# The second batch's column of token 512: its two rounded parts from ScalarE instead of VectorE

## The chip, the cores and the metric

The kernel runs on one core of one Trainium2 chip. The metric is the device time of the whole kernel in microseconds (us). An execution is compared with others of the same kernel and with the kernel before; the profile is one further execution, recorded by the hardware profiler.

The engines are called TensorE (PE in the profile; PEld is its weight load), VectorE (DVE), ScalarE (ACT), GpSimd (POOL) and SyncE (SP, which here only issues transfers). Each works through its own queue of instructions in order.

## The reference

One encoder layer is applied to two batches of 1024 tokens by 1024 channels (`x_prompt` and `x_sample`, in the kernel batch 0 and batch 1). What matters here is its first branch: the normalized input is projected, and a Fourier transform over the tokens and over the 256 channels of each group follows.

```python
def encoder_layer(x, g_pre, w_in, ...):
    xn = rmsnorm(x, g_pre)
    p = xn @ w_in
    fv, fg, hv, hg, mg = jnp.split(p, [...], axis=-1)
    fz = fv.astype(jnp.float32).reshape(B, L, F_GROUPS, F_GROUP_DIM)
    fz = jnp.fft.fftn(fz, axes=(1, 3), norm="ortho").real
    fz = fz.reshape(B, L, F_WIDTH).astype(dt)
    y_f = (fz * jax.nn.silu(fg)) @ w_fourier_out
    ...
    out = (g_f * y_f + g_h * y_h) @ w_out
    return x + rmsnorm(out, g_post)
```

The rest is a convolution branch with filters that are computed in the frequency domain, two gates and an output projection.

## The kernel before

All large products are made in a split form. An fp32 operand is stored as two rounded parts: a high part (a copy that rounds to the type fp32r) and a low part (the operand less its high part, rounded in the same way). A product is then three matmuls, high by high, high by low and low by high (`mm3`, L465). The helper `split` (L167) makes both parts: the high part on ScalarE or VectorE (L170, L172), the low part as a subtraction on VectorE or GpSimd (through `sub` and `tt`, L180).

The Fourier stage uses the symmetry of the transform: each token column is folded into sums and differences of token t and token 1024 - t. Tokens 0 and 512 are their own mirror images. Token 512 is kept apart, in a small tile `x5` of 128 partitions by 8 channel tiles by 36 columns; for batch b its high part goes to columns b and b + 32, its low part to columns b + 2 and b + 34. TensorE multiplies `x5` with the folded projection weights into a tile of 36 rows (`pfx`, in `fourier_half`).

The two batches come to this stage in different ways. Batch 0 is handled two channel tiles at a time (`two_tiles`), and the two parts of its column are made once for all eight tiles. Batch 1 is handled tile by tile in `xtile`, for k from 0 to 7. Tile k is loaded (`xk`, three buffers, from SyncE's queue), transposed and scaled by eight matmuls with a diagonal matrix into two PSUM tiles (`tpx`, from a ring of four that the projection's `pfv` shares), drained by ScalarE into the tile `xg` (L437, two buffers), and stored to DRAM (`d_x`, L438, the same queue as the loads). Then come the sums (`eo[:, 0]`, VectorE) and differences (`eo[:, 1]`, GpSimd) of the fold, their high part `eh` (ScalarE) and low part `el` (VectorE), and the two parts of token 512's column, both on VectorE. `xg` has two columns behind its 1024 tokens, which a memset on GpSimd (L431) clears.

While `xtile` runs for batch 1, the transform of batch 0's second half is still being made on the same engines (`fourier_half`: the tiles `pse`, `pso`, `sst`, `pp`, `qp`, `pP`, `pQ`, `fPs`, `fPm`, `fA`, `fB`); the projection of batch 1 (`pfv`, `pfx`) follows. Behind the Fourier stage comes the filter stage (`phase_main`), in which the weights of the gates' projections are rounded half a block at a time: loaded to `wr`, high part `wh` on ScalarE, low part `wl` on GpSimd, and used by the matmuls into `pin`.

The order of each engine's queue isn't that of the source. A scheduler builds it from the source's instructions by simulating them against a cost model, so that a small change of the source can move instructions far from it.

Of the kernel before, what the change touches and what calls it, by code (L numbers as in the profile page):

```python
# [9 lines left out]
F32 = mybir.dt.float32  # L10
F32R = mybir.dt.float32r
I32 = mybir.dt.int32
AF = mybir.ActivationFunctionType
# [3 lines left out]
P = 128  # L17
# [143 lines left out]
class K:  # L161
# [262 lines left out]
    def xtile(self, b, k, px, fo):  # L424


        nc, a = self.nc, self.a
        xt = px.tile([P, 8, P], F32, tag="x", name=f"xk{b}_{k}", bufs=3)
        nc.sync.dma_start(xt, a[f"x{b}"].rearrange("(m p) c -> p m c", p=P)[:, :, k * P:(k + 1) * P])
        xg = px.tile([P, L + 2], F32, tag="xg", name=f"xg{b}_{k}", bufs=2)  # L430
        nc.gpsimd.memset(xg[:, L:L + 2], 0.0)  # L431
        for n in range(2):
            tp = self.psum("mm", 4, "tpx")
            for q in range(4):
                m = 4 * n + q
                self.mm(tp[:, q * P:(q + 1) * P], xt[:, m], self.diag[:, m], True, True)
            nc.scalar.activation(xg[:, 512 * n:512 * n + 512], tp, AF.Copy, scale=self.gpre[:, k:k + 1])  # L437
        nc.sync.dma_start(self.d_x[b][k], xg[:, 0:L])  # L438
        eo = px.tile([P, 2, 2, 256], F32, tag="eo", name="eo", bufs=2)
        fw = xg[:, 0:512].rearrange("p (a r) -> p r a", r=2)  # L440
        bw = xg[:, 1024:512:-1].rearrange("p (a r) -> p r a", r=2)
        self.add("dve", eo[:, 0], fw, bw)
        self.sub("pool", eo[:, 1], fw, bw)
        self.split(fo["eh"][:, k], fo["el"][:, k], eo, "dve", "act")
        x5 = fo["x5"][:, k]
        self.split(x5[:, b:b + 33:32], x5[:, 2 + b:35 + b:32], xg[:, 512:513].to_broadcast([P, 2]), "dve", "dve")


    def open_weights(self, pw):
# [1133 lines left out]
```

## Time and profile before

| what | value |
| --- | --- |
| median of three runs | 2414.27 us (2414.0 to 2417.5) |
| the profiled execution | 2412.46 us, of which span 2410.7 us |
| mean granted TensorE clock | 0.998 |
| columns of batch 1 (`xtile`) | about 104 to 142 us |
| filter stage | about 202 to 660 us |

The span is the time from the profile's first instruction to its last. A row of the profile names a source line, an engine, an operation, the tiles written and read (buffer numbers left out), the shape, and how often; in a list of instructions in order of time the first two numbers are start and duration in us, and a bracket at the end holds the idle time of the engine before it and what ended it. In a list of groups the numbers behind the bar are busy us, mean ns of one, and idle us before them with what ended most of it. A row of a list of waits reads: engine, tile and line that waited, what for, us in total, times, longest. Where one tile's instructions are listed, three durations in ns are the shortest, the median and the longest. Durations of neighbours on one engine overlap a little at their ends.

### The profile page before, as it was taken

The numbers are of one execution on the slowest core, as the hardware profiler recorded it, in microseconds if no ns is written. First come the engines' busy times: TensorE is split into PE (matmuls) and PEld (weight loads), VectorE is DVE, ScalarE is ACT, GpSimd is POOL, SyncE is SP. The second block draws the span as 40 slices with busy tenths as digits, with TensorE's granted clock in tenths as the row PEclk, the third lists the DMA queues.
The fourth block names the chain that finished last, engine by engine and source line by source line (L and its number), as shares of the span: only waits on it lengthen the run. The fifth ranks groups of instructions, "written<-read, shape, count | busy, mean of one in ns | idle before, by whom it ended". The sixth has DMA issues, their size and how long they took to land.

```text
span 2410.7 us, 36396 instructions
## 1 busy us (share of the span) xinstructions
PE 2368.0 (98%) x13000; PEld 2056.8 (85%) x13000; DVE 1903.5 (79%) x3393; ACT 1073.0 (45%) x2038; POOL 509.2 (21%) x526
## 2 busy tenths in 40 slices
PE   6999999999999999999999999999999999999998
PEld 5998888888888888888888888888888888888886
DVE  7876988888759999999889999867555456665677
ACT  6646666677533333333223223333444444444443
POOL 3341222222242334441000000112100111212111
PEclk9999999999999999999999999999999999999999
DMA  8636655555555455545444444445454667776543
GB/s 262 213 127 220 212 174 170 168 166 162 189 189 183 158 187 175 172 155 195 148 131 140 131 149 135 136 131 184 162 166 157 206 214 256 252 262 216 162 158 131
DMA packets 228464, 428.33 MB, mean 178 GB/s; under 512 B 23286, under 2 KB 89176, under 8 KB 228026
## 3 DMA queue, kind: packets, MB, share of 16 engines
q1 hardware_dynamic: 200493, 333.03, 43.0%
q0 software_dynamic: 27568, 92.94, 11.2%
q8 instruction: 102, 1.67, 0.3%
q14 instruction: 80, 0.66, 0.1%
q10 hardware_dynamic: 221, 0.04, 0.0%
HBM read 290.12 MB, written 135.79 MB: 177 GB/s over the span
## 4 chain that ended last, share of the span: by engine, by line
PE 53%; DVE 0%; DMA 0%; issue 0%; DVEq 0%; ACT 0%; ACTq 0%
PE pin L193 16%; PE pg L193 8%; PE pyh L193 7%; PE pyf L193 7%; PE po L193 6%; PE pT L193 4%; PE pX L193 4%; PE tph L895 1%; DMA wh<-d_w 0%; DVE o L176 0%; DVE xl L180 0%; DVE yc L180 0%; DVE t L180 0%; DVE rs_t L246 0%; DVE rs L247 0%
## 5 line engine op out<-in xcount | busy, mean ns | idle before, releaser
L193 PE MATMUL pin<-xh,wl 128*128 128x512 f32 x1472 | 576.3, 392 | 1.6 <-POOL wl L180 1.6
L193 PE MATMUL pin<-xh,wh 128*128 128x512 f32 x1472 | 576.1, 391 | 1.5 <-DMA wh<-d_w 1.2
L193 PE MATMUL pin<-xl,wh 128*128 128x512 f32 x1472 | 576.4, 392 | 1.1 <-DVE xl L180 0.9
L180 POOL TENSOR_TENSOR wl<-wr,wh 128x512 fp32r<-128x512 f32 x136 | 251.9, 1853 | 1142.0 <-ACT wh L170 1092.3
L193 PEld LDWEIGHTS pin<-xh,wh 128*128 128x128 f32 x1472 | 277.0, 188 | 55.0 <-DMA wh<-d_w 2.1
L193 PEld LDWEIGHTS pin<-xl,wh 128*128 128x128 f32 x1472 | 277.0, 188 | 54.0 <-DVE xl L180 2.2
L193 PEld LDWEIGHTS pin<-xh,wl 128*128 128x128 f32 x1472 | 277.0, 188 | 53.8 <-POOL wl L180 2.6
L170 ACT CAST wh<-wr 128x512 fp32r<-128x512 f32 x264 | 163.5, 619 | 321.7 <-PE pin L193 94.9
L193 PE MATMUL pX<-bh,cfwd 128*128 128x256 f32 x768 | 161.9, 289 | 0.2 <-DVE t L180 0.2
L180 DVE TENSOR_TENSOR t<-pX,k 128x1024 f32<-128x1024 f32 x128 | 155.4, 1214 | 5.6 <-PE pX L193 3.7
L180 DVE TENSOR_TENSOR wl<-wr,wh 128x512 fp32r<-128x512 f32 x128 | 88.0, 687 | 91.0 <-ACT wh L170 90.7
L193 PE MATMUL pyf<-sf,wh 128*128 128x512 f32 x512 | 157.5, 389 | 0.0
L193 PE MATMUL pyh<-sh,wh 128*128 128x512 f32 x512 | 157.2, 389 | 0.0
L193 PE MATMUL pT<-cinv,yh 128*128 128x256 f32 x768 | 145.6, 284 | 0.0
L170 ACT CAST bh<-b 128x512 fp32r<-128x512 f32 x144 | 88.8, 620 | 112.1 <-DVE b L180 77.5
L193 PEld LDWEIGHTS pX<-bh,cfwd 128*128 128x128 f32 x768 | 126.6, 190 | 2.8 <-DVE t L180 0.6
L193 PEld LDWEIGHTS pT<-cinv,yh 128*128 128x128 f32 x768 | 123.1, 190 | 6.7
L170 ACT CAST yh<-y 128x512 fp32r<-128x512 f32 x96 | 59.5, 620 | 138.8 <-DVE y L180 136.3
L193 PEld LDWEIGHTS pyh<-sh,wh 128*128 128x128 f32 x512 | 96.1, 188 | 19.9
L193 PEld LDWEIGHTS pyf<-sf,wh 128*128 128x128 f32 x512 | 96.1, 188 | 19.8
L193 PE MATMUL pT<-cinv,yl 128*128 128x256 f32 x384 | 109.4, 285 | 0.1
L193 PE MATMUL pX<-bl,cfwd 128*128 128x256 f32 x384 | 108.7, 283 | 0.6 <-DVE bl L180 0.6
(374 smaller groups left out, 5313.4 us busy)
## 6 DMA issues: line engine op xcount, KB each, us to landing
k<-d_k SPq DMA_DIRECT2D x128, 512.0 KB, 4.1
wr<-in_w_in SPq DMA_DIRECT2D x136, 256.0 KB, 3.1
d_g<-gt SPq DMA_DIRECT2D x124, 256.0 KB, 2.7
d_k<-kt SPq DMA_DIRECT2D x128, 128.0 KB, 2.2
d_k<-kt SPq DMA_DIRECT2D x64, 256.0 KB, 2.4
wr<-in_w_fo POOLq DMA_DIRECT2D x64, 256.0 KB, 4.1
g<-d_g SPq DMA_DIRECT2D x64, 256.0 KB, 4.0
wr<-in_w_ho POOLq DMA_DIRECT2D x64, 256.0 KB, 3.7
```

What stands on the lines that cost most here:

```text
L170: self.rounded = nc.scalar.copy(h, src)
L180: return e.tensor_tensor(out, a, b, op=op)
L193: return self.nc.tensor.matmul(out, lhsT, rhs, start=start, stop=stop, skip_group_check=shared)
L895: nc.tensor.transpose(tp[:, q * P:(q + 1) * P], eo[:, e, q], self.ident)
```

## The change

In `xtile`, the call of `split` with both parts on VectorE becomes two instructions of ScalarE: a copy that rounds (the high part), and an activation with the function Identity, a scale of -1 and the column as its bias, which gives the column less the high part and rounds it (the low part). Each writes two columns of 128 partitions, as before. Nothing else is edited.

```diff
         self.split(fo["eh"][:, k], fo["el"][:, k], eo, "dve", "act")
         x5 = fo["x5"][:, k]
-        self.split(x5[:, b:b + 33:32], x5[:, 2 + b:35 + b:32], xg[:, 512:513].to_broadcast([P, 2]), "dve", "dve")
+        hi = x5[:, b:b + 33:32]
+        nc.scalar.copy(hi, xg[:, 512:513].to_broadcast([P, 2]))
+        nc.scalar.activation(x5[:, 2 + b:35 + b:32], hi.bitcast(F32), AF.Identity, bias=xg[:, 512:513], scale=-1.0)
```

VectorE's queue has 16 instructions fewer (3379 for 3395 in the program), ScalarE's 16 more (2010 for 1994); the other three queues hold the same instructions. In the scheduled program the order differs from TensorE's 666th to its 3717th matmul, and on the other engines over the corresponding part; before and behind it is the same.

## The prediction

> **What bounds the kernel now.** I read the page's busy times first, then the list of waits for TensorE over the whole span, then the stretch in which the edited lines run.
>
> ```profile
> span 2410.7 us, 36396 instructions
> PE 2368.0 (98%) x13000; PEld 2056.8 (85%) x13000; DVE 1903.5 (79%) x3393; ACT 1073.0 (45%) x2038; POOL 509.2 (21%) x526
> ```
>
> TensorE (PE) is busy for 98% of the span. The change gives it no work and takes none from it, so the time can move only through its idle time, 2410.7 - 2368.0 = 42.7 us in all, or through its clock. The edited lines run once for each of the eight column tiles of the second batch, between 104 and 142 us. The next fence has the table of stretches (PE, PEld, DVE, ACT and POOL busy with their counts, then granted clock, DMA share, GB/s) and TensorE's waits in the first stretch and in the other two.
>
> ```profile
> 104.00:142.00 38.00, 34.29 (x277) 33.55 (x276) 35.20 (x61) 24.09 (x40) 19.96 (x16) 0.96 0.70 236
> 142.00:202.00 60.00, 59.88 (x493) 58.51 (x492) 37.47 (x98) 23.45 (x60) 18.13 (x22) 1.00 0.35 120
> 202.00:660.00 458.00, 455.56 (x2513) 395.92 (x2512) 388.69 (x871) 314.27 (x672) 115.00 (x69) 1.00 0.57 181
> ...
> PE tpx L193 <- DMA xk<-in_x: 2.1, 1, 2.1
> PE pQ L193 <- DVE qp L180: 1.1, 1, 1.1
> PE pfv L193 <- ACT xg L437: 0.6, 1, 0.6
> ...
> PE pin L193 <- POOL wl L180: 1.6, 2, 0.9
> ```
>
> From 104 to 142 us TensorE loses 38.00 - 34.29 = 3.71 us, in the three waits of the list; VectorE (DVE) is the busiest engine beside it, 35.20 of 38.00. From 142 to 202 us TensorE has no wait worth naming. In the filter stage, 202 to 660 us, it loses 2.4 us, of which 1.6 us are two waits for GpSimd (POOL).
>
> **What is removed.** Sixteen VectorE instructions on 128x2 elements, a cast and a subtraction for each tile.
>
> ```profile
> L180 DVE TENSOR_TENSOR x<-xg,x 128x2 fp32r<-128x2 f32 x8 | 6.2, 779 | 0.0
> L172 DVE CAST x<-xg 128x2 fp32r<-128x2 f32 x8 | 3.9, 489 | 0.0
> ...
> 114.22 1.95 DVE L180 TENSOR_TENSOR eo<-xg 128x512 f32<-128x512 f32 x1
> 116.09 1.48 DVE L172 CAST x<-xg 128x2 fp32r<-128x2 f32 x1
> 117.60 0.16 DVE L180 TENSOR_TENSOR x<-xg,x 128x2 fp32r<-128x2 f32 x1
> 117.68 0.69 DVE L180 TENSOR_TENSOR qp<-sst,qp 128x514 fp32r<-128x514 f32 x1
> 118.28 0.69 DVE L180 TENSOR_TENSOR eo<-xg 128x512 f32<-128x512 f32 x1
> ...
> 121.68 1.46 DVE L180 TENSOR_TENSOR x<-xg,x 128x2 fp32r<-128x2 f32 x1
> ```
>
> ```profile
> 113.51 0.10 POOL L431 MEMSET xg<- 128x2 f32 x1 [2.71 <-DMA d_x<-xg]
> 113.57 3.97 POOL L180 TENSOR_TENSOR eo<-xg 128x512 f32<-128x512 f32 x2
> ```
>
> They hold VectorE for 6.2 + 3.9 = 10.1 us, far more than two elements a lane need. The cast at 116.09 ends at 117.57, where GpSimd ends its pair of subtractions `eo` (113.57 + 3.97 = 117.54); the next operation of the same shape, at 117.60, takes 0.16 us. So most of that time is VectorE held off until GpSimd is done. It isn't a property of the small operations: the 128x512 `eo` at 114.22 took 1.95 us where the one at 118.28 took 0.69. In the changed order of VectorE the instruction behind `eo` is again one with both inputs in SBUF (px, qp, el) behind tiles 0, 1, 2, 4, 5 and 6, and inherits the hold; only behind tiles 3 and 7 is it a drain of PSUM. I count as freed the own work, 16 x 0.16 us = 2.6 us, and the holds of those two tiles (1.46 - 0.16 us at 121.68, and as much again): 5 of the 10.1 us.
>
> The Trainium skill (SBUF — State Buffer, section "Who interferes with whom") says that a VectorE instruction with two SBUF inputs and a GpSimd instruction that reads SBUF exclude each other for a whole instruction. By it the hold goes to the next such instruction in the queue, which speaks against the change; the 1.95 us above agree. Taken for every instruction behind `eo`, it would keep tile 3's 1.46 us too and make the sum 0; the section exempts an instruction with a single SBUF input, as the drains of PSUM are, and with that it is the sum below.
>
> **What is added.** Sixteen ScalarE instructions on 128x2. The trace has the nearest row at the same shape, the copy of L362.
>
> ```profile
> L362 ACT COPY r<-xg x8: 190/193/207, 23.4 to 54.9; 128x2 f32<-128x2 f32 x8
> 122.90 0.36 ACT L577 COPY fPs<-pP 128x256 f32<-128x256 f32 x1
> 115.70 0.49 ACT L578 ACTIVATE fPm<-pP,vec 128x258 f32<-128x258 f32 x1
> ```
>
> The copy costs 0.19 us. The activation with a bias at this shape isn't in the trace: at least 0.19 us, at most the 0.49 us of L578's activation on 258 columns; I take 0.20, as it is nearer in shape. That makes 8 x (0.19 + 0.20) = 3.1 us, at most 5.4 us, in a stretch where ScalarE is idle for 38.00 - 24.09 = 13.9 us. No table load is added in the changed order. Without that cover, each pair would put 0.4 us before an eviction of `xg`.
>
> **What is late next.** The longest of the three waits decides.
>
> ```profile
> 115.57 0.34 SPq L438 DMA_DIRECT2D d_x<-xg  x1
> 116.00 0.46 SPq L429 DMA_DIRECT2D xk<-in_x  x1
> ...
> 122.32 0.69 ACT L437 ACTIVATE xg<-tpx,gpre 128x512 f32<-128x512 f32 x1 [2.18 <-DMA d_x<-xg]
> ...
> 118.42 0.51 PE L193 MATMUL pQ<-qp,chan 128*128 128x258 f32 x2 [1.09 <-DVE qp L180]
> ...
> 123.84 3.24 PE L193 MATMUL tpx<-dg,xk 128*128 128x128 f32 x16 [2.05 <-DMA xk<-in_x]
> ...
> q1 hardware_dynamic: 4991, 4.85, 97.1%
> ```
>
> TensorE waits until 123.84 for the load of tile 6, issued at 116.00. The store of tile 2, issued 0.43 us ahead of it in the same queue, landed only at 122.32, 6.75 us after its issue, and from 112 to 128 us (the fence's last row, from the DMA queues of that stretch) this queue's packets fill 97.1% of the DMA engines. The load is held by transfers, not by VectorE. The wait of 1.09 us for `qp`, ahead of it, goes: GpSimd's next `eo` now stands behind the memset of tile 3, which waits for a store of tile 1 as that of 113.51 did for tile 0's, so `qp` is free to run behind `eo`, at about 114.22 + 1.95 = 116.2. But TensorE only reaches tile 6 earlier and waits there longer. Worth 0, bounds 0 and -1.09 us.
>
> SyncE's queue itself sees one delay. Tile 2's second eviction now stands behind the two drains of pP (0.36 + 0.49 = 0.85 us), so that tile's store and the load of tile 6 are issued up to 0.85 us later. Bounds 0 and +0.85 us; I take 0, as the queue has two older transfers under way. Tile 7's load is issued about 1 us earlier and lands no sooner, for the same reason.
>
> Then the wait of 0.57 us ahead of the first `pfv`:
>
> ```profile
> 125.96 5.12 POOL L180 TENSOR_TENSOR eo<-xg 128x512 f32<-128x512 f32 x2 [0.73 <-DVE x L172]
> ...
> 129.04 1.05 ACT L170 CAST eh<-eo 128x1024 fp32r<-128x1024 f32 x1 [0.66 <-DVE x L180]
> ...
> 130.26 1.27 ACT L437 ACTIVATE xg<-tpx,gpre 128x512 f32<-128x512 f32 x2
> ...
> 128.49 1.95 PE L193 MATMUL tpx<-dg,xk 128*128 128x128 f32 x16
> 131.01 0.51 PE L193 MATMUL pfv<-we,eh 128*128 128x260 f32 x2 [0.57 <-ACT xg L437]
> ```
>
> `pfv` needs a PSUM buffer that ScalarE drains at 130.26, behind the cast `eh` of 129.04, which waits for tile 4's `eo`. GpSimd starts that one at 125.96, after VectorE's `el` of tile 2 has freed its buffer. Without the 1.46 us of tile 3 ahead of it, that `el` runs some 1.5 us earlier, the chain follows, and the drain comes at about 129 us, ahead of the end of TensorE's `tpx` (128.49 + 1.95 = 130.44). The wait goes: -0.57 us. TensorE is bound by its own work behind it, so the gain carries on to the end.
>
> **Further on.** The list of instructions differs in its order on every engine up to TensorE's 3717th matmul of 12584, near 650 us, and is the same behind that. In the filter stage instructions of VectorE move by about ten places and the rounding of weights on ScalarE by up to 19. I counted, for each of the 60 weight halves of this stage, TensorE's work between the last matmul for which ScalarE's queue up to their rounding waits and their first use, with 0.23 us from matmul to matmul:
>
> ```profile
> 689.71 0.39 PE L193 MATMUL pin<-xh,wh 128*128 128x512 f32 x1
> 689.93 0.39 PE L193 MATMUL pin<-xl,wh 128*128 128x512 f32 x1
> ```
>
> 8 halves of before, and 10 of after, have less than 8 us. With the slack alike I take 0 for this part, bounds -1.6 (both waits gone) and +6.4 us (rival 4).
>
> **The sum.** 0 - 0.57 + 0 + 0 = -0.57 us. The profiled execution took 2412.46 us, 1.76 us beside its span, and would take 2411.9; the median of the runs, 2414.27, lies 1.8 us above it, so the forecast there is 2413.7 us, with 2412.6 to 2414.6 as its own range (the bounds -1.09 and +0.85 us above).
>
> **The rivals.** 1. VectorE's freed 5 us come through: tile 6 lands earlier, since stores leave earlier, and all three waits and the slow clock behind them go.
>
> ```profile
> 122.00:124.00 2.00, 0.16 (x1) 0.19 (x2) 2.00 (x4) 1.68 (x4) 1.16 (x2) 1.00 0.95 288
> 124.00:126.00 2.00, 2.00 (x12) 2.00 (x12) 2.00 (x5) 2.00 (x4) 0.14 (x2) 0.60 0.80 278
> 126.00:128.00 2.00, 2.00 (x12) 2.00 (x11) 2.00 (x3) 0.63 (x2) 2.00 (x1) 0.55 0.90 311
> ```
>
> After the idle stretch the granted clock is 0.60 and 0.55 for 4 us, which costs 4.00 - 2.00 x (0.60 + 0.55) = 1.70 us. All together -(1.09 + 2.05 + 0.57 + 1.70) = -5.4: 2408.9 us. The full DMA queue speaks against it.
>
> 2. The clock keeps up: the idle time now comes in two pieces (tile 5's load, then tile 6's), and the dip stays away: -0.57 - 1.70 = -2.3: 2412.0 us.
>
> 3. The clock drops once more or for longer and tile 6 comes 0.85 us later: -0.57 + 0.85 + 1.70 = +2.0: 2416.3 us. The Trainium skill (TensorE: Matmul & The Clock Gate, section "What's actually happening") has the clock halved after an idle window of about 3.4 us that runs free of the program; by it rivals 2 and 3 hang on where the window falls, each at 1.70 us for a window won or lost, and the 4 us here agree.
>
> 4. The slower side: the new order starves GpSimd's rounding of weights in the filter stage.
>
> ```profile
> L180 POOL TENSOR_TENSOR wl<-wr,wh 128x512 fp32r<-128x512 f32 x136 | 251.9, 1853 | 1142.0 <-ACT wh L170 1092.3
> ...
> 456.71 5.43 POOL L180 TENSOR_TENSOR wl<-wr,wh 128x512 fp32r<-128x512 f32 x1 [8.46 <-ACT wh L170]
> ```
>
> A `wl` that meets a run of VectorE's two-input work takes up to 5.43 us where the page's mean is 1.853. Two waits cost 1.6 us, 0.8 each; if all ten tight halves waited so, 8.0 - 1.6 - 0.57 = +5.8: 2420.1 us. It decides from one further wait on (0.8 against 0.57). Against it: of the 60 halves of before, 8 of them tight, two waited.
>
> 5. The change does nothing in the end: the drain at 130.26 stays where it is, as the added instructions in ScalarE's queue take back what VectorE gives. 2414.3 us.
>
> **How the numbers follow.** Forecast 0.37, rival 1 0.10, rival 2 0.12, rival 3 0.15, rival 4 0.18, rival 5 0.08. About 0.2%, 4.8 us, is what a measurement of this kernel tells from no change. Beyond it on the fast side lies rival 1 and a little of rival 2: 0.11. On the slow side most of rival 4 and a little of rival 3: 0.15. Within: 0.74. The range goes from rival 1 to rival 4, 2409 to 2420 us.
>
> **What would show it.** Right: no `x` of VectorE between 104 and 142 us; the copies at 0.19 us and the activations at about 0.2; `qp` of 117.68 near 116.2; TensorE still waits for tile 6 until 122.3 to 124.7; the first `pfv` at about 130.5 with no wait; two or three waits for `wl`. Wrong: tile 6 started before 122 us (rival 1), a granted clock of 1.00 from 124 to 128 us (2) or below it for over 5 us (3), four or more waits for `wl` in the filter stage (4), and above all a difference that arises behind 660 us, where the orders agree and I allow nothing.

## The result, and the profile after

The changed kernel takes 2417.85 us (median of 21 runs, 2414.58 to 2421.62), the kernel before, run beside it, 2412.92 us (21 runs, 2409.43 to 2417.96). The ratio is 1.0020, with a 95% interval from 1.0015 to 1.0026: the change costs some 4.9 us, where 0.57 us of gain was forecast. The profiled execution of the changed kernel took 2414.58 us, its fastest, so its profile can't show all of the loss.

The page of the changed kernel, span and busy times:

```profile
span 2412.8 us, 36397 instructions
PE 2368.4 (98%) x13000; PEld 2057.6 (85%) x13000; DVE 1895.1 (79%) x3377; ACT 1075.4 (45%) x2054; POOL 503.9 (21%) x526
```

TensorE is as busy as before (2368.4 us for 2368.0). Its table of stretches (columns as in the prediction) tells where its idle time lies:

```profile
104.00:142.00 38.00, 35.35 (x293) 34.06 (x292) 33.55 (x51) 27.70 (x60) 17.40 (x18) 1.00 0.69 240
142.00:202.00 60.00, 59.85 (x492) 58.49 (x491) 35.94 (x94) 23.73 (x60) 18.57 (x21) 1.00 0.40 136
202.00:660.00 458.00, 450.91 (x2482) 392.11 (x2482) 385.64 (x869) 312.41 (x669) 112.52 (x67) 1.00 0.55 178
```

In the stretch that holds the edited lines TensorE is idle for 38.00 - 35.35 = 2.65 us, 1.06 us less than before, and its clock is 1.00 where it was 0.96. In the filter stage, where nothing is edited, it is idle for 458.00 - 450.91 = 7.09 us; before it was 2.44, so 4.65 us are lost there.

That a gain of 1.06 us, a clock dip of 1.70 us that stays away and a loss of 4.65 us add up to +1.9 us, near the two spans' difference of 2.1 us, is partly chance, as these terms aren't all. The changed kernel has a dip of its own in the filter stage: the granted clock is 0.79, 0.50 and 0.86 in the three stretches of 2 us from 212 to 218 us, which costs 1.70 us again; in the kernel before it is 1.00 there. The filter stage can also be timed as a whole, from the first matmul into `pin` (at 202.08 us before, 200.50 after) to the first one from which on TensorE's order is the same again (657.02 and 660.98 us). It lasts 460.48 us instead of 454.94, 5.54 us more. The changed kernel comes to it 1.58 us sooner, and takes 1.85 us less behind it.

The list of TensorE's waits for the whole span names what it waited for there (total, times, longest):

```profile
PE pin L193 <- POOL wl L180: 3.1, 1, 3.1
PE tpx L193 <- DMA xk<-in_x: 2.4, 4, 1.3
PE pin L193 <- ACT xh L170: 1.6, 1, 1.6
...
PE pXf L193 <- ACT kt L806: 1.4, 1, 1.4
```

The filter stage has one long wait for GpSimd's `wl` instead of two short ones, and two waits for ScalarE, for `xh` and `kt`. The list of instructions in order of time shows the first of the three, on VectorE, GpSimd and TensorE of the changed kernel:

```profile
249.52 0.27 DVE L764 TENSOR_SCALAR T<-T,vec 128x128 f32<-128x128 f32 x1
249.72 0.68 DVE L180 TENSOR_TENSOR xp<-fE 128x512 f32<-128x512 f32 x1
...
257.22 0.75 DVE L180 TENSOR_TENSOR b<-xm,bs 128x256 f32<-128x256 f32 x2
258.32 1.32 DVE L180 TENSOR_TENSOR bl<-b,bh 128x512 fp32r<-128x512 f32 x1 [0.35 <-ACT bh L170]
...
250.68 10.12 POOL L180 TENSOR_TENSOR wl<-wr,wh 128x512 fp32r<-128x512 f32 x2 [1.18 <-ACT wh L170]
...
259.15 0.50 PE L193 MATMUL pin<-xh,wl 128*128 128x512 f32 x1 [3.15 <-POOL wl L180]
```

The view of the tile `wl` between 244 and 265 us gives the shortest, median and longest of three, in ns:

```profile
L180 POOL TENSOR_TENSOR wl<-wr,wh x3: 1292/1730/8418, 245.0 to 259.1; 128x512 fp32r<-128x512 f32 x3
```

The `wl` that starts at 250.68 takes 8.418 us. In that time VectorE runs additions and subtractions of two inputs in SBUF without a break, from 249.72 until it waits 0.35 us for a `bh`, ahead of 258.32. The `wl` ends at 250.68 + 8.42 = 259.10, which is 1.13 us behind the beginning of that gap (258.32 - 0.35 = 257.97), and TensorE goes on at 259.15. In the kernel before, the scaling of T stood inside such a run:

```profile
250.99 2.60 POOL L180 TENSOR_TENSOR wl<-wr,wh 128x512 fp32r<-128x512 f32 x1
...
252.36 1.31 DVE L762 TENSOR_SCALAR T<-T,vec 128x128 f32<-128x128 f32 x1
```

There the `wl` ended at 253.59, 1.23 us behind the start of the scaling. In the changed order the scaling (L764, the same instruction) is done at 249.52, ahead of the run and of the `wl`.

The other two waits are for ScalarE. The rows of ScalarE, and TensorE's two waits, in the changed kernel:

```profile
207.97 1.28 ACT L747 ACT_TABLE_LOAD   x1
209.26 1.71 ACT L747 ACTIVATE ex<-dec,vec 128x256 f32<-128x256 f32 x4
210.88 1.03 ACT L170 CAST xh<-xl 128x1024 fp32r<-128x1024 f32 x1
...
369.56 1.28 ACT L882 ACT_TABLE_LOAD   x1
...
372.47 0.31 ACT L806 ACTIVATE kt<-kt 128x128 f32<-128x128 f32 x1
...
211.96 0.51 PE L193 MATMUL pin<-xh,wh 128*128 128x512 f32 x1 [1.63 <-ACT xh L170]
...
372.84 0.36 PE L193 MATMUL pXf<-bh,cfwd 128*128 128x256 f32 x1 [1.43 <-ACT kt L806]
```

A table load and four `ex` stand ahead of the `xh` that TensorE wants, and a table load ahead of the `kt`. For the `kt` this is new: from 360 to 374 us the kernel before loads a table once, the changed kernel three times. For the `xh` it isn't. In the kernel before the same load and the same `ex` stand ahead of it, and it runs later, but TensorE has 18 matmuls (into `pft` and `pQ`) between its `pP` at 211.34 and the matmul that needs the `xh`; in the changed order that matmul comes directly behind `pP`. The kernel before:

```profile
213.49 1.03 ACT L170 CAST xh<-xl 128x1024 fp32r<-128x1024 f32 x1
...
214.57 1.02 PE L193 MATMUL pin<-xh,wh 128*128 128x512 f32 x2 [0.28 <-ACT xh L170]
```

### The profile page after: what moved, and what is told of

It is laid out like the page before. It is cut to its first block, busy times and chain, and to the rows that moved or that the text cites. A ratio compares the mean times of both kernels' runs of the same rounds, so it can differ in the third digit from the quotient of the medians.

```text
span 2412.8 us, 36397 instructions
## 1 busy us (share of the span) xinstructions
PE 2368.4 (98%) x13000; PEld 2057.6 (85%) x13000; DVE 1895.1 (79%) x3377; ACT 1075.4 (45%) x2054; POOL 503.9 (21%) x526
## 4 chain that ended last, share of the span: by engine, by line
PE 56%; DVE 1%; DMA 0%; issue 0%; DVEq 0%; ACT 0%; ACTq 0%
PE pin L193 18%; PE pg L193 8%; PE pyh L193 7%; PE pyf L193 7%; PE po L193 6%; PE pT L193 4%; PE pX L193 4%; PE tph L897 1%; DMA wh<-d_w 0%; DVE b L180 0%; DVE t L180 0%; DVE o L176 0%; DVE yl L180 0%; DVE y L180 0%; DVE T0s L180 0%
```

## The experiments

The theory, called the order theory: the loss arises between 200 and 660 us from the order in which the scheduler puts the unedited instructions there. Its rivals: the arithmetic theory (the sixteen operations on ScalarE cost it) and the clock theory (ordinary executions run at a lower granted clock than the one profiled). Every difference below is against the kernel before, run beside it on the same chip, as the ratio times 2413 us, with its interval.

| run | what | median, us | difference, us | TensorE idle 202 to 660 us |
| --- | --- | --- | --- | --- |
| e1 | the changed kernel again | 2418.82 | +6.3 (3.6 to 8.9) | 7.97 |
| e2 | the edit, old order | 2411.93 | -1.2 (-3.4 to 1.0) | 2.52 |
| e3 | old arithmetic, new order | 2418.55 | +5.1 (2.7 to 7.5) | 7.96 |
| e4 | the edit, new order to 200 us, then old | 2412.97 | -0.7 (-2.9 to 1.4) | 2.58 |
| e5 | old arithmetic, old order to 200 us, then new | 2420.92 | +7.0 (4.8 to 9.2) | 7.83 |
| e6, e11 | high part only on ScalarE | 2409.91, 2410.66 | -3.4 (-5.5 to -1.4), -2.9 (-5.1 to -1.0) | 3.06, 2.04 |
| e7 | low part only on ScalarE | 2419.44 | +6.3 (4.1 to 8.4) | 7.94 |
| e8 | changed kernel, one move | 2413.87 | +1.2 (-1.0 to 3.1) | 3.92 |
| e9 | changed kernel, three moves | 2411.59 | -2.2 (-4.3 to 0.0) | 2.89 |
| e10, e12 | kernel before, one move | 2413.38, 2413.00 | +0.5 (-1.7 to 2.7), -1.4 (-3.6 to 0.7) | 2.12, 2.05 |
| e13 | kernel before, two moves | 2418.28 | +4.1 (1.9 to 6.5) | 5.73 |

**e1: the changed kernel again.**

> The changed kernel once more, beside the kernel before, for a second profile. Its first profile (2414.58 us) was the fastest of its 21 runs and 3.3 us under their median, so it can't show all of the loss of 4.9 us. Order theory (the loss arises between 200 and 660 us, from the new order of the instructions there, not from the sixteen edited ones): median 2416 to 2419 us, and TensorE again idle for 6 to 9 us between 202 and 660 us (2.4 us in the kernel before), with a wait of about 3 us for wl near 255 us. Arithmetic theory (ScalarE's sixteen added operations cost it): the idle time is in 104 to 142 us, more than 3.7 us. Clock theory (typical runs have a lower granted clock than the one profiled): the idle time is that of the first profile, and the granted clock is below 1.00 in some further stretch, worth 2 to 3 us.

The median is 2418.82 us, and the table of stretches has

```profile
202.00:660.00 458.00, 450.03 (x2491) 391.25 (x2490) 384.92 (x869) 313.20 (x669) 114.51 (x67) 1.00 0.55 179
```

The idle time in the filter stage is there again, with the same waits of 3.1, 1.6 and 1.4 us, and two waits for `xl` of 1.7 us together; the granted clock behind the wait for `wl` was 1.00 in both profiles. The loss is a fixed pattern, not an accident of one execution.

**e2 to e5: arithmetic and order taken apart.** The order is held by order-only edges between neighbours of each engine's queue, from a list of the instructions in the wanted order (the code is shortened here: in the kernel the list is unpacked from a string). In e2 and e4 this is added to the changed kernel, in e3 and e5 to the kernel before; only the list differs:

```diff
+def _pin(tc):
+    made = {int(i.name[2:]): i for i in tc.nc.cur_bb.bb.instructions}
+    last = {}
+    for n in order:
+        ins, prev = made[n], last.get(made[n].engine)
+        if prev is not None:
+            tc.add_manual_dep(ins, prev.name, DependencyInfo(NoSync, DATA), reason="pin")
+        last[ins.engine] = ins
...
         _body(tc, a)
+        _pin(tc)
```

> The edit, with every engine's instructions held in the order of the kernel before (the sixteen edited ones move to ScalarE at their old place). Order theory: no loss, 1 to 3 us faster than the kernel before, TensorE idle between 202 and 660 us 2 to 3 us. Arithmetic theory: still 4 to 5 us slower. Clock theory: 2 to 3 us slower, with a granted clock under 1.00 where the kernel before has 1.00.

> The kernel before in its arithmetic (both parts on VectorE), with every engine's instructions held in the order of the changed kernel. Order theory: 4 to 6 us slower than the kernel before (it has the loss between 202 and 660 us and at most some of the gain before 142 us). Arithmetic theory: within 1 us of the kernel before. Clock theory: within 1 us too.

> The edit, in the changed kernel's own order up to the start of the filter stage at about 200 us, and in the order of the kernel before from there on. Order theory: the gain ahead of 142 us stays (1.8 us at the first pfv in the first profile) and the loss goes: 1.5 to 3 us faster than the kernel before, TensorE idle between 202 and 660 us about 2.4 us. Arithmetic theory: 4 to 5 us slower. Clock theory: 2 to 3 us slower.

> The kernel before in its arithmetic, in its own order up to the start of the filter stage at about 200 us, and in the changed kernel's order only from there on. Nothing of the edit runs, and nothing ahead of 200 us differs from the kernel before. Order theory: the whole loss, 4.5 to 6 us slower than the kernel before, TensorE idle 7 to 8.5 us between 202 and 660 us with the waits 3.1 (wl), 1.6 (xh) and 1.4 us (kt) at the same places. Arithmetic theory: within 1 us of the kernel before. Third theory, that the loss is made ahead of 200 us and only shown behind: within 1 us too.

The stretch of the filter stage in the tables of e2 and of e5:

```profile
202.00:660.00 458.00, 455.48 (x2506) 395.69 (x2505) 388.34 (x869) 313.41 (x670) 118.19 (x70) 1.00 0.56 181
```

```profile
202.00:660.00 458.00, 450.17 (x2484) 391.39 (x2483) 383.71 (x866) 311.52 (x667) 114.28 (x67) 1.00 0.55 179
```

The time goes with the order and not with the arithmetic. The edit in the old order isn't slower (e2, e4: the intervals hold 0). The kernel before in the new order loses the whole amount (e3), and it does so when nothing but the order behind 200 us is new (e5): not one edited instruction and none ahead of 200 us differs there. The length of the filter stage between the two matmuls named above says the same: 460.2 to 461.8 us in the five profiles with the new order (the changed kernel, e1, e3, e5, e7), 454.5 to 455.8 us in the seven with the old one (the kernel before, e2, e4, e6, e10, e11, e12). Behind it all 15 profiles take 1751.8 to 1756.7 us, whichever the order. The list of waits of e5 is that of the changed kernel:

```profile
PE pin L193 <- POOL wl L180: 3.1, 1, 3.1
PE pin L193 <- ACT xh L170: 1.6, 1, 1.6
PE pin L193 <- DVE xl L180: 1.6, 2, 0.9
PE pXf L193 <- ACT kt L804: 1.4, 1, 1.4
```

The arithmetic theory falls. The clock theory falls as a rival (it expected e2 and e4 slower), but a part of it stays as a sequel of the wait. Behind the `wl` wait of e5, and not in the two profiles of the changed kernel, the table has

```profile
262.00:264.00 2.00, 2.00 (x7) 1.57 (x6) 0.00 (x0) 0.00 (x0) 0.27 (x1) 0.53 0.53 197
264.00:266.00 2.00, 2.00 (x7) 1.54 (x6) 0.00 (x0) 0.00 (x0) 0.00 (x0) 0.62 0.09 33
```

The column behind POOL's count is the granted clock: 4.00 - 2.00 x (0.53 + 0.62) = 1.70 us are lost, the very amount of the dip near 126 us in the kernel before. Three of the five profiles with this 3.1 us wait have such a dip behind it (e3, e5, e7); a fourth, the first of the changed kernel, has its dip behind the wait for `xh`. None of the seven profiles with the old order has one between 202 and 660 us. So an execution of the new order loses some 5 us in waits and often 1.70 us more.

**e6, e7, e11: one part alone.** Here nothing is pinned; the scheduler orders each program itself.

```diff
-        nc.scalar.copy(hi, xg[:, 512:513].to_broadcast([P, 2]))
-        nc.scalar.activation(x5[:, 2 + b:35 + b:32], hi.bitcast(F32), AF.Identity, bias=xg[:, 512:513], scale=-1.0)
+        self.split(hi, x5[:, 2 + b:35 + b:32], xg[:, 512:513].to_broadcast([P, 2]), "dve", "act")
```

(e6 and e11; e7 keeps the activation and makes the cast with VectorE's tensor_copy.)

> Only the high part (the cast) made by ScalarE, the low part left on VectorE as a subtraction; the scheduler orders the program itself. From 200 us on it comes out in the order of the kernel before. Order theory: 0 to 3 us faster than the kernel before. Arithmetic theory: about half of the loss, 2 to 3 us slower.

> Only the low part (the activation with the bias) made by ScalarE, the cast left on VectorE; the scheduler orders the program itself. From 200 us on it comes out in the order of the changed kernel. Order theory: the whole loss, 4 to 6.5 us slower than the kernel before, with the same three waits. Arithmetic theory: about half of the loss, 2 to 3 us slower.

> The kernel with only the high part made by ScalarE once more, since it came out 3.4 us faster than the kernel before, with an interval from 1.4 to 5.5 us. If that holds: 2409 to 2412 us, 1.4 to 4 us faster than the kernel before, and a granted clock of 1.00 between 124 and 128 us. If it was a lucky set of runs: within 1 us of the kernel before.

Neither part costs half. The edit of eight instructions that leaves the old order of the filter stage is 3.4 and 2.9 us faster than the kernel before, the edit of the other eight, which comes out in the new order, 6.3 us slower. The high part alone is faster than the kernel before, twice, with intervals that leave out 0. By the traces it gains ahead of the filter stage: from the first `tpx` matmul of batch 1 to the first into `pin` TensorE takes 96.30 us (e6) and 97.54 us (e11), where the kernel before takes 99.34; but e2 and e4 take as little, 96.85 and 97.68 us. Its gain isn't explained as well as the loss: e6 has no dip of the clock near 126 us, but e11 has it (0.53 and 0.62 from 124 to 128 us) and is as fast; and why the high part alone came out better than both parts in the old order (e2, e4) isn't settled, as the intervals overlap.

**e8: the run of VectorE broken.** The changed kernel in its own order, VectorE's queue with one move:

```diff
 L180 acc<-acc,ex
-L764 T<-T,vec
 L180 xp<-fE
 L180 xm<-fE
 L180 xp<-fO
 L180 xm<-fO
 L180 acc<-acc
 L180 b<-xp
+L764 T<-T,vec
 L180 fE<-T
```

> The changed kernel in its own order, but for one VectorE instruction, the scaling of T on 128x128 (one tensor input, at 249.52 us of the first profile), which is moved six places back, into the run of two-input instructions behind it. Order theory with its mechanism (GpSimd's wl of 250.68 us takes 8.42 us because it is held off by a run of VectorE instructions with two inputs in SBUF): that wl ends at its first gap, in about 3 us instead of 8.42, the wait of 3.1 us for it goes, and the time falls by 2.5 to 5 us from the changed kernel, to 2413 to 2416 us. Rival, that wl is slow for another reason (its load, DMA traffic): wl stays above 6 us and the time within 1 us of the changed kernel's 2418.

VectorE and GpSimd in the list by time of e8:

```profile
253.67 1.31 DVE L764 TENSOR_SCALAR T<-T,vec 128x128 f32<-128x128 f32 x1
...
251.75 3.15 POOL L180 TENSOR_TENSOR wl<-wr,wh 128x512 fp32r<-128x512 f32 x1 [1.08 <-ACT wh L170]
```

The `wl` takes 3.15 us instead of 8.42 and ends at 254.90, 1.23 us behind the start of the scaling. The wait of 3.1 us is gone, the two of ScalarE are still there, and the median is 2413.87 us, some 5 us under e1: one 128x128 instruction moved by six places takes most of the loss back. That is more than the wait itself. A dip that no longer follows it may make up the rest; this isn't shown, as neither profile of the changed kernel had a dip behind that wait. Between the two matmuls the filter stage of e8 lasts 457.11 us, with a dip behind the wait for `xh` that is left.

**e9: all three waits.** The move of e8 on VectorE, and two on ScalarE:

```diff
+L170 xh<-xl
 L747 ex<-dec,vec (x4, with the table load ahead of it)
-L170 xh<-xl
...
-L747 ex<-dec,vec (x4)
 L792 kt<-kt
...
 L806 kt<-kt
+L747 ex<-dec,vec (x4)
```

> The changed kernel in its own order with three moves in the filter stage, of work that delays what TensorE waits for: the scaling of T on VectorE as in the run before; on ScalarE the first cast xh of the second four tiles (210.88 us of the first profile) ahead of the four ex and their table load; and on ScalarE four ex (367.52 us) behind the kt of 372.47, which takes two of the 23 table loads away. Order theory: the waits of 3.1 (wl), 1.6 (xh) and 1.4 us (kt) go, TensorE is idle for 1 to 2.5 us between 202 and 660 us, and the kernel is 1 to 4 us faster than the kernel before. If the moves only shift the waits (another buffer is late next): idle time above 4 us, and a time within 1 us of the run with one move, 2414 us.

TensorE's waits from 200 to 662 us:

```profile
PE pft L193 <- ACT sev L538: 1.6, 1, 1.6
PE pin L193 <- DVE xl L180: 0.8, 1, 0.8
PE pin L193 <- POOL wl L180: 0.4, 1, 0.4
```

The three waits are gone. One of 1.6 us for `sev`, which now stands behind the `xh` and the `ex` in ScalarE's queue, is new, so that 2.89 us of idle time stay, a little over what was expected. At 2411.59 us the kernel is 2.2 us faster than the kernel before, with an interval that just reaches 0. Its filter stage lasts 454.59 us, as in the old order. The two moves on ScalarE weren't run apart from each other.

**e10, e12, e13: the run made in the kernel before.** If the run is the cause, it must cost time with nothing of the edit. In e10 the scaling of T was moved ahead, to directly behind the `T` that it scales, in e12 to behind the first `xm` of the run. The queue of e10:

```diff
 L180 T<-pft,ex
+L762 T<-T,vec
...
 L180 acc<-acc,ex
-L762 T<-T,vec
```

> The kernel before in its own order, but for one VectorE instruction: the scaling of T on 128x128, which stands at 252.36 us of its profile inside a run of two-input instructions and behind the start of the wl of 250.99 us, is moved eight places ahead, out of the run. Order theory with its mechanism: that wl, 2.60 us before, now takes 6 to 9 us, a wait for wl of 2 to 4 us appears near 258 us, in about half of the executions with a lower granted clock behind it (worth 1.7 us), and the time rises by 2 to 5 us over the kernel before. Rival, that the run of two-input instructions isn't what holds wl: wl stays below 4 us and the time within 1 us of the kernel before.

> The run before this with the move mended: there the scaling of T had to wait 1.73 us for ScalarE's ex, left VectorE idle, and GpSimd slipped in, so that the long run never met the wl. Now, in the kernel before, the scaling of T is moved only five places ahead, behind the first xm (about 250.3 us), where ex is done and wl (250.99 us) hasn't begun. Order theory with its mechanism: that wl takes 6 to 9 us instead of 2.60, TensorE waits 2 to 4 us for it near 258 us, in some executions with a lower granted clock behind it (1.7 us), and the time is 2 to 6 us over the kernel before; nothing of the edit is in this kernel. Rival: wl below 4 us, the time within 1 us of the kernel before. If the scaling comes so late that it falls on the start of wl, wl takes 2 to 3 us and nothing is told.

Neither tells anything of the `wl` it was aimed at. In both the scaling had to wait for ScalarE's `ex` (1.73 and 0.20 us) and fell on the start of that `wl`, which took 1.3 us. But the following `wl` met the run in their place. GpSimd and VectorE in e12:

```profile
256.75 4.92 POOL L180 TENSOR_TENSOR wl<-wr,wh 128x512 fp32r<-128x512 f32 x1 [3.89 <-ACT wh L170]
...
260.88 1.33 DVE L180 TENSOR_TENSOR bl<-b,bh 128x512 fp32r<-128x512 f32 x1 [0.35 <-ACT bh L170]
```

It ended at 261.67, 1.14 us behind the beginning of the gap of 0.35 us (260.53). No matmul was waiting for it, and it cost nothing. e13 moves the scaling, and the `fE` that reads it, behind the run:

```diff
 L180 acc<-acc,ex
-L762 T<-T,vec
 L180 b<-xp
...
-L180 fE<-T
 L180 b<-bs
...
 L180 bl<-b,bh
+L762 T<-T,vec
+L180 fE<-T
 L759 RECIPROCAL
```

> The kernel before in its own order, but for two VectorE instructions: the scaling of T on 128x128 (252.36 us of its profile) and the fE that reads it (255.61 us) move back, behind the second bl (260.54 us). What is left between 249 and 257 us are instructions with two inputs in SBUF with nothing between them, and the wl of 250.99 us meets them from its start. Order theory with its mechanism: that wl takes 6 to 9 us instead of 2.60 and ends about 1.1 us behind the first moment in which VectorE is idle (near 257 us, where a bl waits for ScalarE's bh); TensorE, which needs it 24 matmuls ahead of 260.14 us, waits 2.5 to 4.5 us for it; the time is 3 to 7 us over the kernel before, at the upper end where the granted clock falls behind the wait (1.7 us). Rival, that the run isn't what holds wl: wl below 4 us, the time within 1.5 us of the kernel before.

GpSimd, VectorE and TensorE of e13, then the row of the tile `wl` between 244 and 265 us:

```profile
251.53 8.93 POOL L180 TENSOR_TENSOR wl<-wr,wh 128x512 fp32r<-128x512 f32 x2
...
258.01 1.32 DVE L180 TENSOR_TENSOR bl<-b,bh 128x512 fp32r<-128x512 f32 x1 [0.35 <-ACT bh L170]
...
258.84 0.79 PE L193 MATMUL pin<-xh,wl 128*128 128x512 f32 x1 [3.58 <-POOL wl L180]
```

```profile
L180 POOL TENSOR_TENSOR wl<-wr,wh x3: 1415/1714/7249, 244.8 to 258.8; 128x512 fp32r<-128x512 f32 x3
```

Two moved VectorE instructions turn the `wl` of 2.60 us into one of 7.25. It ends at 251.53 + 7.25 = 258.78, again 1.12 us behind the beginning of the gap (257.66), and TensorE waits 3.58 us where it had waited for nothing. The kernel before becomes 4.1 us slower, with none of the change in it. The cause of the longest wait is shown from both sides, by e8 and by e13.

## Why the prediction was wrong

The step that failed is "Further on": "With the slack alike I take 0 for this part." It measured 4.65 us of idle time in the first profile and 5.5 in the second (455.56 - 450.03), and 5.3 to 6.9 us by the length of the filter stage in the five profiles of the new order; e5 shows that it is the whole loss. The count behind it looked at one thing, how much of TensorE's work lies between the matmul that frees ScalarE's queue up to a rounding and the first use of that weight half. That leaves out what the new order changed: which run of VectorE a `wl` meets on its way, how much work TensorE has left ahead of the matmul that needs an `xh`, and where a table load falls ahead of a `kt`. `xh` and `kt` aren't weight halves and weren't counted at all.

Rival 4 had the place and the agent: GpSimd's `wl`, starved by VectorE's two-input work in the filter stage. Its price, +5.8 us, was near the measured loss by luck: it was built from ten short waits of 0.8 us, and the run shows one of 3.15 us and two for ScalarE. Its sign ("four or more waits for `wl`") didn't show, though its mechanism did. The prediction knew that a `wl` can take 5.43 us and set 0.8 us as the price of one; it didn't ask, for the order at hand, how long the run is that each `wl` would meet. That could be read beforehand: between the scaling of T and the next instruction of VectorE that isn't a two-input one, the reciprocal, the changed order has 21 instructions.

The other steps:

- Removed: near in size. Up to the first matmul into `pin` VectorE has the 16 instructions fewer and is busy for 151.63 - 146.78 = 4.85 us less, beside the 5 us counted as freed; the other half of the 10.1 us went to other instructions, as said. The kernel before, then the changed one (columns as in the tables above):

```profile
0.00:202.08 202.08, 175.95 (x1383) 168.66 (x1383) 151.63 (x361) 115.75 (x239) 71.93 (x91) 0.99 0.60 201
0.00:200.50 200.50, 176.48 (x1382) 168.43 (x1383) 146.78 (x345) 117.67 (x254) 69.97 (x91) 0.99 0.60 205
```

- Added: the copy is at its 0.19 us; the activation was mis-sized, 0.20 us taken, 0.30 measured, within its bounds. The groups of the changed kernel (busy us, mean ns):

```profile
L448 ACT ACTIVATE x<-x,xg 128x2 fp32r<-128x2 f32 x8 | 2.4, 301 | 0.0
L447 ACT CAST x<-xg 128x2 fp32r<-128x2 f32 x8 | 1.5, 193 | 0.1
```

  The Trainium skill (ScalarE: Activation LUTs, section "What ACT_TABLE_LOAD costs") gives about 280 ns plus 0.83 ns per element for an activation whose bias is read from a tile, 282 ns here as an estimate; the trace agrees nearly, with 301. That ScalarE hides the sum of 3.9 us is borne out by e2 and e4, which aren't slower.
- What is late next: right. These are `qp` on VectorE, and on TensorE tile 6 (with its wait for the load) and the first `pfv`:

```profile
115.16 1.14 DVE L180 TENSOR_TENSOR qp<-sst,qp 128x514 fp32r<-128x514 f32 x1 [0.79 <-ACT qp L170]
...
123.16 1.13 PE L193 MATMUL tpx<-dg,xk 128*128 128x128 f32 x8 [1.35 <-DMA xk<-in_x]
...
129.17 0.51 PE L193 MATMUL pfv<-we,eh 128*128 128x260 f32 x2
```

  `qp` came 1 us sooner than said (116.2), tile 6 waited for its load until 123.16, inside the 122.3 to 124.7 of the prediction, and `pfv` started at 129.17 without a wait (130.5 was said). In e1 that wait is back, 0.9 us: it varies between executions.
- The clock: rival 2's condition came true. The kernel before has a mean granted clock of 0.96 from 104 to 142 us, and so have e5, e10, e12 and e13, which are that kernel in its own order there; in the changed kernel and all the runs with both edited parts (e1, e2, e4, e8, e9) it is 1.00, and so it is in e3, which has the new order and the old arithmetic. So locally the edit gains about what rival 2 said: 1.06 + 1.70 us by the tables of the two kernels, 99.34 - 97.38 = 1.96 us from the first `tpx` matmul of batch 1 to the first into `pin`, and 1.2 and 0.7 us by the medians of e2 and e4, which can't be told from 0. It was outweighed.

## What to carry to other kernels

When an edit passes through a scheduler that orders the queues anew, the edited instructions are the smaller question: compare the two orders and price what moved. For each GpSimd operation that reads SBUF, go along VectorE's queue from its start to the next idle moment or instruction without two SBUF inputs, and compare that with the time at which its result is needed; on ScalarE look at what a table load comes to stand ahead of, and on TensorE at how much work is left ahead of the matmul that needs the result. And before a source change is judged by its time, run it once with the old order held: here the same edit is no slower or 5 us slower by the order alone.

## What the runs showed of the hardware

- A GpSimd operation that reads SBUF didn't get a turn between VectorE's two-input instructions, however many there were. Undisturbed such a `wl` takes 1.29 us; it took 2.60, 3.15, 4.92, 7.25 and 8.42 us, and ended 1.1 to 1.2 us behind the first gap of VectorE, though the gap was only 0.35 us long, or behind the start of the TENSOR_SCALAR. The Trainium skill (SBUF — State Buffer, section "Who interferes with whom") has the second of two such instructions blocked until the first has finished. By that, as an estimate, one 0.68 us instruction would be the most; in the changed kernel it was over 7 us (250.68 to 257.97), in which 18 instructions of VectorE were let in ahead of the waiting `wl`. The measurement decides.
- The TENSOR_SCALAR in which `wl` slips in pays for it: 1.31 us in e8 and in the kernel before, 0.27 us where no GpSimd operation is under way (249.52 in the changed kernel). So it isn't free of the conflict but is the one that yields, where the prediction took instructions with a single SBUF input as exempt.
- A wait of TensorE of 3.1 us is sometimes followed by a slower clock and sometimes not, with the same order and the same wait: in three of five profiles, each time at 1.70 us (in e3, 0.60 and 0.55 from 260 to 264 us). The wait of 1.6 us for `xh` was followed by one in the first profile of the changed kernel and in e8 (0.73, 0.50 and 0.92 from 214 to 220 us), and by none in e1, e3, e5 and e7; it is shorter than the idle window that rival 3 goes by. Behind the 3.58 us of e13 the clock was at 0.50 for longer:

```profile
258.00:260.00 2.00, 1.16 (x3) 0.97 (x4) 1.99 (x2) 0.00 (x0) 2.00 (x2) 0.50 1.14 400
260.00:262.00 2.00, 2.00 (x7) 1.51 (x6) 1.24 (x2) 0.00 (x0) 0.47 (x1) 0.50 0.97 339
262.00:264.00 2.00, 2.00 (x6) 1.61 (x5) 0.00 (x0) 0.00 (x0) 0.00 (x0) 0.50 0.42 150
264.00:266.00 2.00, 2.00 (x9) 1.57 (x9) 0.00 (x0) 0.00 (x0) 0.00 (x0) 0.83 0.00 0
```

  From TensorE's restart at 258.84 that is 0.50 x (1.16 + 2.00 + 2.00) + 0.17 x 2.00 = 2.9 us. So a wait can cost nearly twice its length.
